# One diffusion layer with a state-space mixer: eigenvalues on half the columns, modulation by halves, states in four blocks

## Chip, core and metric

The kernel runs on one core of one Trainium2 chip. The time is device time of one execution in microseconds (us). Before the change: median 1114.01 of three runs, 1113.48 to 1120.88.

Five engines work beside each other, each in its own order: TensorE (PE; PEld is its weight load), VectorE (DVE), ScalarE (ACT), GpSimd (POOL), and SyncE (SP), which only issues transfers. An instruction waits by semaphores for what it needs, and all that stands behind it on its engine waits with it.

## The reference

One layer, 1024 latent tokens and 256 context tokens, 1024 channels. Everything is float32.

```
m_l, m_c = silu(c) @ ada_w + ada_b, silu(c_ctx) @ ada_w + ada_b      # six vectors of 1024 each
h = rms_norm(x) * (1 + scale) + shift                                # tokens and context, own vectors
# S5: 64 groups of 16 channels, 64 complex states per group, 2 directions
lam_bar = exp(lam * exp(log_step));  b_bar = (lam_bar - 1) / lam * b
h_t = lam_bar * h_{t-1} + b_bar @ u_t;  y_t = Re(c @ h_t)            # over the context, then over the tokens
y = gelu(y_fwd + y_bwd + d * h);  y = y * sigmoid(y @ w_glu + b_glu)
x = x + gate * y
x = x + gate2 * (silu(h2 @ w1) * (h2 @ w3)) @ w2                     # h2: modulated norm of x, hidden 2816
out = rms_norm(x) * norm_final
```

## The kernel before, in words

Eight consecutive tokens form a chunk: 128 chunks of latent tokens and 32 of context. `U` holds tokens transposed, 128 partitions (8 tokens x 16 channels), 64 groups, 160 chunks (`Xc` the 32 of context, `X` the 128 of tokens). The order of the work is written out by hand: the tile library adds the waits, it does not move instructions. Regions of SBUF (`R0`, `RA`, `RU`, `RC[0..3]`, `RXa`, `RXc`) are divided by hand and used several times.

1. **Squares and eigenvalues** (lines 159 to 277). ScalarE squares ten strips, GpSimd adds the two halves of each (line 165), TensorE sums over partitions (166). Beside it VectorE works out exp and sine of the eigenvalues as polynomials, on 128 partitions x 128 columns: 64 states, held twice in the partitions, by 2 directions x 64 groups. `PW` becomes powers 1 to 8 of the eigenvalues, `CP` those times (lam_bar - 1)/lam, by complex products `cmul` (247). `LB` is the table of `CP` in both directions, with signs, copied by ScalarE (276, 277).
2. **Modulation** (`ada1`, `mix_cols`, `u_ctx`, `rs_lat`, `u_lat`). `ada1(k)` multiplies 128 rows of the first 2048 columns of ada_w, from four buffers of 1 MB; `mix_cols` turns the result into columns for all 64 groups. `rs_lat` scales a block of 8 groups by 1/rms on VectorE; `u_lat` modulates it, odd blocks on VectorE, even ones group by group on ScalarE (398); `u_ctx` does the context on GpSimd.
3. **Input matrices.** A half block `hb` is 8 groups in one direction: b = hb // 2, d = hb % 2. `bl_make(hb)` forms two products of 1024 elements of `BXY` and `LB`, on GpSimd for `PMUL`, else on VectorE. `bl_tr` transposes their sum into `Win`: for hb < `NPE` TensorE adds while transposing (343, 344), for the others an accumulating transfer issued by GpSimd adds first (`bl_sum`, 333). `lb_psum` copies parts of `LB` to PSUM, for the VectorE ones. `ada(n)` multiplies tiles of 256 KB of the rest of ada_w, up to tile n of 64; `ada_load` issues their loads on SP, through 16 first and then 8 buffers.
4. **The loop over 16 half blocks** (552 to 583). `sums(hb)`: 32 matrix products and their copies into `ST`, states of all 160 chunks. Behind it in each iteration: `bl_tr(hb + 3)`, `bl_sum(hb + 6)`, `bl_make(hb + 7)`, modulation of block hb + 2, `pair(hb - 1)` (a step of the scan within pairs of chunks, on GpSimd for `PPAIR`). `powers` makes the eigenvalues to the 8th, 16th ... 128th (`SQ`, in PSUM `LQ`). `ctx_low` combines the context's chunks in pairs and fours, quarter by quarter; after the loop `ctx_high` finishes the tree for all at once.
5. **Scan** (`scan`, 641). VectorE: 32 double steps and 63 single ones over all 64 state columns of `ST` (`STE`), with `fill_ops` for two of the four quarters in between; the other two by `fill` on GpSimd.
6. **`run`** (759): a written program for everything beside the scan: A = `ada`, C = output tables by `cl_gen`, K = `k_mats` (kernel matrices; ScalarE copies them at 622 and sends them out), T = `toeplitz` (reads them back), R = `restack` (719, ScalarE copies states for TensorE; the first one is R0), P and Y = products and their copies, F = `fill`, L, G, B, M, Z smaller ones.
7. From line 799 on: the rest of the outputs, the GLU, and the feed-forward network on TensorE.

All of VectorE's and GpSimd's elementwise operations of two tensors stand in the profile under the helper's line 70.

Of the kernel before, what the change touches and what calls it, by code (L numbers as in the profile page):

```python
# [17 lines left out]
P = 128  # L18
# [19 lines left out]
def s5_ffn_kernel(tc, a, out):  # L38
# [3 lines left out]
    with ctx:  # L42
# [67 lines left out]
        ST = view(RA, 0.5, [160, 2, 2, 32])  # L110
        STE = view(RA, 0.5, [160, 2, G])
# [18 lines left out]
        lamp = view(RA, 0, [3, P])  # L130
# [5 lines left out]
        ctxT = view(RA, 40, [G, 32])  # L136
# [6 lines left out]
        stage = [view(RA, 48 + 8 * i, [2048]) for i in range(4)]  # L143
        adaw = a["ada_w"]
        for k in range(4):
            SY.dma_start(stage[k], adaw[k * P:(k + 1) * P, 0:2048])


        def t_(i):
            return view(RA, 1.5 + 0.5 * i, [P])  # L150
# [10 lines left out]
        for i in range(10):  # L161
            src = X[:, 8 * i:8 * i + 8] if i < 8 else ctxT[:, 32 * i - 256:32 * i - 224]
            jk, po = junk[i % 2], psx if i < 8 else psc
            S.activation(jk.rearrange("p a b -> p (a b)").rearrange("p (g c) -> p g c", c=src.shape[2]), src, AF.Square)
            tt(jk[:, 0], jk[:, 0], jk[:, 1], ADD, E)
            PE.matmul(po.rearrange("p g c -> p (g c)"), blk, jk[:, 0], start=i % 8 == 0, stop=i in (7, 9))
# [57 lines left out]
        PW = view(RXa, 0, [8, 2, P])  # L224
        CP = view(RA, 12, [T, 2, P])
# [3 lines left out]
        cmt = view(RXc, 0, [512])  # L229
        yb = LTb[:, 0:256].rearrange("p (r n) -> p r n", r=2)  # L230
        rsp, rcp, colp = LTb[:, 256:384], LTb[:, 384:416], LTb[:, 384:512].rearrange("p (b g) -> p b g", b=2)
# [15 lines left out]
        def cmul(o, x):  # L247

            m = x.shape[1]
            a_, b_ = (t[:, :256 * m].rearrange("p (m r n) -> p m r n", m=m, r=2) for t in (LTa, cmt))  # L250
# [11 lines left out]
        cmul(CP[:, 2:4], CP[:, 0:2])  # L262
        V.tensor_reduce(rsx, psx.rearrange("p g c -> p c g"), AX.X, ADD)
        V.tensor_reduce(rsc, psc.rearrange("p g c -> p c g"), AX.X, ADD)
        S.activation(rsb, rsb, AF.Sqrt, bias=epsc[:, 0:1], scale=1.0 / D)
        cmul(PW[:, 2:3], PW[:, 0:1])
        V.tensor_copy(yb, PW[:, 3])
        cmul(CP[:, 4:6], CP[:, 0:2])
        V.reciprocal(rsp, rsx)
        V.reciprocal(rcp, rsc)  # L270
        cmul(CP[:, 6:8], CP[:, 2:4])
        LB = view(RC[2], 8, [2, T, P])
        for d in range(2):
            sl = slice(64 * d, 64 * d + 64)
            cp_ = CP[:, ::-1, :, sl] if d == 0 else CP[:, :, :, sl]
            S.copy(LB[:, 0, :, sl], cp_[:, :, 0])
            S.activation(LB[:, 1, :, sl], cp_[:, :, 1], AF.Copy, scale=sgn[:, 0:1])

        LH = view(RXc, 0, [2, 3, G])
        SQ = [LS[:, 0], view(RXc, 2, [3, G]), LH[:, 0], LH[:, 1], LS[:, 1]]  # L280

        def powers():

            for gp in range(2):
                o = LS[64 * gp:64 * gp + 64, 0]
                v = PW[64 * gp:64 * gp + 64, 7].rearrange("p r (d g) -> p r d g", d=2)[:, :, :, gp::2]
                S.copy(o[:, 0::2].rearrange("p r (d g) -> p r d g", d=2), v)
                S.activation(o[:, 1].rearrange("p (d g) -> p d g", d=2), v[:, 1], AF.Copy, scale=-1.0)
            tq = view(RXc, 3, [2, G])
            for p in range(4):  # L290
                i_, o = SQ[p], SQ[p + 1]
                if p < 2:
                    V.tensor_copy(LQ[p], i_)
                j_ = LQ[p] if p < 2 else i_
                tt(tq, i_[:, 0:2], j_[:, 0::2], MUL)
                stt(o[:, 1], i_[:, 0], -2.0, j_[:, 2], MUL, MUL)
                stt(o[:, 2], i_[:, 0], 2.0, j_[:, 2], MUL, MUL)
                tt(o[:, 0], tq[:, 0], tq[:, 1], ADD)
# [4 lines left out]
        BL2 = [view(r, kb, [8, T, HC]) for r, kb in ((RC[1], 12), (RXc, 4), (RC[3], 4), (RA, 24), (RA, 28), (RA, 32))]  # L303
# [18 lines left out]
        def lb_psum():  # L322

            for n, hb in enumerate((4, 6, 7, 9, 11, 12, 14)):
                bank, o = ((LTa, 384), (tq, 256), (tq, 384), (lbt, 0), (lbt, 128), (lbt, 256), (lbt, 384))[n]
# [28 lines left out]
        def ada1(k):  # L354
            st = stage[k % 4]
            if k >= 4:
                SY.dma_start(st, adaw[k * P:(k + 1) * P, 0:2048])
            for i in range(4):
                PE.matmul(prow[32 * i:32 * i + 2], scs[:, k], st[:, i * 512:(i + 1) * 512], start=k == 0, stop=k == 7,
                          tile_position=(0, 32 * i))  # L360

        def mix_cols():
            cb = LTa[:, 0:32].rearrange("p (r b j) -> p r b j", r=2, b=2)
            mx = view(RXc, 1, [2, 2, G])
            r4 = view(RXc, 2, [4, P])
            S.copy(r4, prow.rearrange("p (m n) -> p m n", m=4))
            pt = pw()
            for m in range(4):
                PE.transpose(pt[:, m], r4[:, m], ident)
            for r in range(2):  # L370
                tt(cb[:, r].rearrange("p b (j m) -> p b j m", m=4),
                   pt.rearrange("p m (b j q) -> p b j m q", b=2, j=2)[:, :, :, :, r],
                   modb[:, 0:2].rearrange("p b (j m) -> p b j m", m=4), ADD)
            stt(cb[:, :, 1], cb[:, :, 1], 1.0, bc(nrm[:, 0], 1, 2), ADD, MUL)
            tt(mx.rearrange("p r b (j g) -> p (r b j) g", g=T), bc(cb.rearrange("p r b j -> p (r b j)"), 2, T), bc(msk, 1, 32), MUL)
            pcol = pw([2, 2, G])
            PE.matmul(pcol, sel, mx, start=True, stop=True)
            PE.matmul(colp, sel, mx[:, 0], start=True, stop=True)
            S.copy(cols, pcol)
# [11 lines left out]
        def u_lat(b):  # L391
            gs = slice(8 * b, 8 * b + 8)
            if b % 2:
                tt(X[:, gs], X[:, gs], bc(colp[:, 1, gs], 2, P), MUL)
                tt(X[:, gs], X[:, gs], bc(colp[:, 0, gs], 2, P), ADD)
            else:
                for g in range(8 * b, 8 * b + 8):
                    S.activation(X[:, g], X[:, g], AF.Identity, bias=cols[:, 0, 0, g:g + 1], scale=cols[:, 0, 1, g:g + 1])


        NA = 16
        stg = [view(RA, i, [512]) for i in (20, 22, 0, 2, 4, 6, 8, 10, 40, 42, 44, 46, 12, 14, 16, 18)] + [view(RC[2], 8 * (1 - i // 4) + 2 * (i % 4), [512]) for i in range(8)]
# [21 lines left out]
        tt(Xc, ctxT, bc(rcp, 1, G), MUL)  # L424
        for k in range(8):
            ada1(k)
        SY.dma_start(BXY[:, 1], a["bxy"][:, 1])
        ada_load(NA)
        bl_make(0)
        bl_make(1)  # L430
        cmul(PW[:, 7:8], PW[:, 3:4])
        rs_lat(0)
        mix_cols()
        tq = pA.tile([P, 512], F32, tag="r3", name="tq")
        lbt = pA.tile([P, 512], F32, tag="r4", name="lbt")
        u_ctx(0)
        rs_lat(1)
        u_lat(0)
        bl_tr(0)
        bl_tr(1)  # L440
        ada(NA // 2, NA)
        lb_psum()
        bl_make(2)
        u_ctx(1)
        u_lat(1)
        bl_make(3)
        bl_tr(2)
        bl_sum(3)
        ada(NA, NA)
# [949 lines left out]
```

## Time and profile before

| | |
|---|---|
| median of 3 runs | 1114.01 us |
| the profiled execution, its own time | 1120.2 us |
| its span | 1118.4 us |
| TensorE busy | 995.1 us, 89% |
| VectorE | 826.2 us, 74% |
| GpSimd | 647.1 us, 58% |
| ScalarE | 414.4 us, 37% |
| first matrix product of the loop's `sums` | 68.4 us |
| first operation of the scan | 149.7 us |
| first restack | 205.0 us |

The span is the time between the first and the last instruction; the profiled execution's own time lies 1.8 us over it, and 6.2 us over the median. Times in the profile count from the span's start. "Busy" is the sum of instruction times without overlap; an engine that is not busy waits, and the bracket behind a row of the timeline says how long and for whom. The matrix products are pipelined, so their single durations overlap. Rows of a product in float32 count two instructions for each call, transposes one.

### The profile page before, as it was taken

What the parts mean: (1) busy time and instruction counts of PE and PEld (TensorE: products, weight loads), DVE (VectorE), ACT (ScalarE), POOL (GpSimd) and SP (SyncE); (2) the same over time, 40 slices, a digit from 0 to 9 for tenths busy, and PEclk for the clock granted to TensorE, in tenths of its full rate; (3) what the DMA queues carried; (4) which work ended last, traced back from release to release, by engine and by line L of the source; (5) the groups of instructions that cost most, each with busy time, mean ns of one, the idle gap of its engine ahead of it and who ended that gap; (6) DMA issues with size and microseconds to landing.
All of it is one profiled execution on the core that took longest, in us unless ns stands there. A gap on an engine that the chain in (4) does not pass through costs nothing.

```text
span 1118.4 us, 16588 instructions
## 1 busy us (share of the span) xinstructions
PE 995.1 (89%) x6104; PEld 804.1 (72%) x6104; DVE 826.2 (74%) x1690; ACT 414.4 (37%) x868; POOL 647.1 (58%) x503
## 2 busy tenths in 40 slices
PE   4687896746969999879999999999999999999997
PEld 1266622636869997667888888888888888888885
DVE  8979899981777787998666766666666666666657
ACT  4267721734834465222222222222222222222236
POOL 4379787865382353865555555555555555555563
PEclk9698997767999999899999999999999999999999
DMA  9956787754421201101111111111111111111114
GB/s 349 343 105 124 193 259 214 174 112 102 152 74 41 76 1 57 57 19 57 57 57 50 32 35 55 57 57 57 57 57 57 57 57 57 57 56 56 37 41 151
DMA packets 51457, 103.64 MB, mean 93 GB/s; under 512 B 4272, under 2 KB 25008, under 8 KB 49328
## 3 DMA queue, kind: packets, MB, share of 16 engines
q1 hardware_dynamic: 43456, 85.67, 23.1%
q0 software_dynamic: 3600, 13.11, 6.3%
q10 hardware_dynamic: 4320, 3.81, 1.1%
q8 instruction: 48, 0.79, 0.3%
q14 instruction: 33, 0.27, 0.1%
HBM read 83.30 MB, written 6.16 MB: 80 GB/s over the span
## 4 chain that ended last, share of the span: by engine, by line
PE 63%; DVE 20%; ACT 5%; DMA 4%; issue 2%; POOL 1%; ACTq 0%; DVEq 0%; SPq 0%; POOLq 0%
PE pu L1109 10%; PE pu L1108 10%; PE pu L1107 10%; DVE ru L70 6%; PE pd L1107 6%; PE pd L1108 6%; PE pd L1109 6%; DVE ra L70 4%; DVE rxa L70 3%; DMA ra<-kd 2%; PE pw L467 2%; PE pe L873 2%; PE pe L872 2%; PE pe L874 2%; PE pw L737 1%
## 5 line engine op out<-in xcount | busy, mean ns | idle before, releaser
L70 POOL TENSOR_TENSOR c<-rxc,c 128x512 fp32r<-128x512 f32 x128 | 169.9, 1342 | 184.6 <-ACT c L1053 175.8
L70 DVE TENSOR_TENSOR ru<-pd,ru 128x512 f32<-128x512 f32 x336 | 227.0, 690 | 2.3 <-PE pd L1109 2.3
L1108 PE MATMUL pu<-ra,c 128*128 128x512 f32 x432 | 168.2, 389 | 0.6 <-DVE ra L70 0.6
L1109 PE MATMUL pu<-ra,c 128*128 128x512 f32 x432 | 168.3, 390 | 0.3 <-POOL c L70 0.3
L1107 PE MATMUL pu<-ra,c 128*128 128x512 f32 x432 | 168.3, 390 | 0.3 <-ACT ra L1053 0.3
L1053 ACT CAST c<-rxc 128x512 fp32r<-128x512 f32 x128 | 76.7, 617 | 185.6 <-POOL rxc L70 107.2
L1107 PE MATMUL pd<-c 128*128 128x512 f32 x336 | 133.3, 397 | 10.9 <-DVE ru L70 10.9
L1108 PE MATMUL pd<-c 128*128 128x512 f32 x336 | 132.5, 394 | 0.0
L1109 PE MATMUL pd<-c 128*128 128x512 f32 x336 | 132.2, 393 | 0.0
L70 DVE TENSOR_TENSOR ru<-pu,ru 128x512 f32<-128x512 f32 x84 | 57.9, 689 | 87.4 <-PE pu L1109 52.6
L70 POOL TENSOR_TENSOR c<-ru,c 128x1024 fp32r<-128x1024 f32 x22 | 53.3, 2424 | 85.9 <-ACT c L851 77.1
L1109 PEld LDWEIGHTS pu<-ra,c 128*128 128x128 f32 x432 | 81.1, 188 | 17.9 <-POOL c L70 1.2
L1108 PEld LDWEIGHTS pu<-ra,c 128*128 128x128 f32 x432 | 81.1, 188 | 17.7 <-POOL c L70 0.9
L1107 PEld LDWEIGHTS pu<-ra,c 128*128 128x128 f32 x432 | 81.1, 188 | 17.5 <-ACT ra L1053 0.8
L1107 PEld LDWEIGHTS pd<-c 128*128 128x128 f32 x336 | 64.1, 191 | 26.2 <-DVE ru L70 12.9
L1109 PE MATMUL pu<-c,c 128*128 128x512 f32 x192 | 74.8, 390 | 0.4 <-POOL c L70 0.4
L1107 PE MATMUL pu<-c,c 128*128 128x512 f32 x192 | 74.9, 390 | 0.0
L1108 PE MATMUL pu<-c,c 128*128 128x512 f32 x192 | 74.7, 389 | 0.0
L1109 PEld LDWEIGHTS pd<-c 128*128 128x128 f32 x336 | 64.2, 191 | 13.6
L1108 PEld LDWEIGHTS pd<-c 128*128 128x128 f32 x336 | 64.2, 191 | 13.2
L70 DVE TENSOR_TENSOR ru<-ru,rxa 128x512 f32<-128x512 f32 (+1 forms) x62 | 62.7, 1011 | 6.7 <-ACT ru L1252 2.7
L70 POOL TENSOR_TENSOR c<-rxc,rxa 128x1024 f32<-128x1024 f32 x30 | 62.1, 2130 | 9.1 <-PE pw L540 4.2
(289 smaller groups left out, 2220.7 us busy)
## 6 DMA issues: line engine op xcount, KB each, us to landing
c<-in_ada_w SPq DMA_DIRECT2D x48, 256.0 KB, 4.9
ru<-in_w SPq DMA_DIRECT2D x22, 512.0 KB, 3.6
c<-c POOLq DMA_DIRECT2D x19, 512.0 KB, 5.9
rxc<-in_w SPq DMA_DIRECT2D x38, 256.0 KB, 4.4
rxc<-in_w SPq DMA_DIRECT2D x19, 512.0 KB, 5.1
ra<-in_ada_w SPq DMA_DIRECT2D x8, 1024.0 KB, 9.8
ru<-in_xT SPq DMA_DIRECT2D x4, 1024.0 KB, 6.4
ra<-in_ada_w SPq DMA_DIRECT2D x16, 256.0 KB, 6.0
```

What stands on the lines that cost most here:

```text
L70: eng.tensor_tensor(out=o, in0=x, in1=y, op=op)
L467: PE.matmul(pv[64 * (i % 2):64 * (i % 2) + 64, i // 2], w[:, i, 64 * ri:64 * ri + 64], U[:, 8 * b + 4 * j + i], start=True, stop=True)
L737: PE.matmul(inner[u][:, i], U[:, 4 * u + i, 32:160], kq, start=i == 0, stop=False)
L872: PE.matmul(pz, h_[:, k], wH[:, k], start=n == 0, stop=False)
L873: PE.matmul(pz, h_[:, k], wL[:, k], start=False, stop=False)
L874: PE.matmul(pz, l_[:, k], wH[:, k], start=False, stop=n == 7)
L1053: S.copy(o[0], x)
L1107: PE.matmul(pu, wh, bh, start=start, stop=False)
L1108: PE.matmul(pu, wh, bl, start=False, stop=False)
L1109: PE.matmul(pu, wl, bh, start=False, stop=stop)
```

## The change

- **Half the columns.** The input `lam` becomes 128 x 3 x 64: a direction in each half of the partitions, where both halves held both. VectorE's eigenvalue operations, `PW` and `CP` have 64 columns. `dup` multiplies with parts of the identity on TensorE and so writes them into both halves of the partitions: for `LB` (four products of 512 columns, copied alternately by ScalarE and VectorE), for the 8th power (`power8`), and for the output tables (`pw_full`, four times, in iterations 5 to 8, into `PWF`). Two complex products of `PW` go from ahead of the loop into iteration 3.
- **Squares.** The addition on GpSimd goes; TensorE takes both halves of each strip, two products instead of one.
- **Modulation by halves.** `ada1(h, k)` takes 512 of the 1024 channels (for shift and scale each); all 16 tiles have a place of their own and are loaded without waiting for one another, half 0 first. `mix_cols` runs for half 0 ahead of the loop and for half 1 in iteration 2. Half 1's products lie ahead of the loop (4) and in iterations 0 and 1.
- **Order ahead of the loop.** Two half blocks instead of three are transposed there; the third goes into iteration 0. Block 0 is modulated half by ScalarE, half by VectorE. Even blocks are modulated by ScalarE in small portions (`UACT`) over iterations 0 to 10.
- **More adding by TensorE** (`NPE` 4 for 3); `PMUL` has 7 entries for 8.
- **ada_w tiles.** 24 buffers first instead of 16. None is multiplied ahead of the loop, 24 in iterations 3 to 9; after the loop 40 follow instead of 48 from iteration 10 on.
- **States in four blocks.** `ST` becomes four separate quarters `STQ`, 20.125 KB apart; `STE` is the view over all.
- **Context tree by blocks.** `ctx_tree` works on one quarter, all levels but the last, in iterations 4 to 15; quarter 0's two lowest levels on GpSimd. After the loop one tree on a quarter of a quarter and `ctx_last`, with all operands for the factors in PSUM (`LQ`), follow.

```diff
+        STB = 20.125
+        STQ = [view(RA, STB * q + 0.125, [160, 2, 2, 8]) for q in range(4)]
+        STE = view(RA, 0, [4, 161, 2, 16]).rearrange("p q c r e -> p c r q e")[:, 1:]
...
-            tt(jk[:, 0], jk[:, 0], jk[:, 1], ADD, E)
-            PE.matmul(po.rearrange("p g c -> p (g c)"), blk, jk[:, 0], start=i % 8 == 0, stop=i in (7, 9))
+            for j in range(2):
+                PE.matmul(po.rearrange("p g c -> p (g c)"), blk, jk[:, j], start=i % 8 == 0 and j == 0, stop=i in (7, 9) and j == 1)
...
+        def ada1(h, k):
+            for b in range(2):
+                i = 2 * b + h
+                PE.matmul(prow[32 * i:32 * i + 2], scs[:, k], stage[h][k][:, b], start=k == 0, stop=k == 7, tile_position=(0, 32 * i))
+        def dup(pt, src):
+            for d in range(2):
+                sl = slice(64 * d, 64 * d + 64)
+                for j in range(2):
+                    PE.matmul(pt[64 * j:64 * j + 64, :, sl], ident[:, sl], src(d), start=True, stop=True)
...
         V.tensor_reduce(rsx, psx.rearrange("p g c -> p c g"), AX.X, ADD)
         V.tensor_reduce(rsc, psc.rearrange("p g c -> p c g"), AX.X, ADD)
         S.activation(rsb, rsb, AF.Sqrt, bias=epsc[:, 0:1], scale=1.0 / D)
...
         cmul(CP[:, 4:6], CP[:, 0:2])
...
         cmul(CP[:, 6:8], CP[:, 2:4])
+        for k in range(3):
+            ada1(0, k)
         LB = view(RC[2], 8, [2, T, P])
+        for n in range(4):
+            i, t0 = n // 2, 4 * (n % 2)
+            pt = pw()
+            dup(pt, lambda d: CP[:, t0:t0 + 4, i] if d else CP[:, ::-1, i][:, t0:t0 + 4])
...
-        PMUL, NPE = (0, 1, 2, 3, 5, 8, 10, 13), 3
+        PMUL, NPE = (0, 2, 5, 6, 8, 10, 13), 4
...
+        lb_psum(1, 3, 4)
         bl_make(0)
         bl_make(1)
+        bl_make(2)
+        V.reciprocal(rsp, rsx)
+        V.reciprocal(rcp, rsc)
+        for k in range(3, 6):
+            ada1(0, k)
+        power8()
         rs_lat(0)
+        tt(Xc, ctxT, bc(rcp, 1, G), MUL)
+        for k in range(6, 8):
+            ada1(0, k)
+        pt = mix_rows()
+        bl_tr(0)
+        mix_cols(0, pt)
+        u_act(0, 0, 4)
+        u_lat(0, 4)
         u_ctx(0)
+        bl_tr(1)
+        bl_make(3)
+        u_ctx(1)
+        for k in range(4):
+            ada1(1, k)
+        SY.dma_start(BXY[:, 0], a["bxy"][:, 2])
+        ada_load(9)
         rs_lat(1)
+        u_lat(1)
+        rs_lat(2)
+        bl_make(4)
+        bl_make(5)
+        bl_sum(4)
...
+        UACT = {0: (2, 0, 2), 1: (2, 2, 5), 2: (2, 5, 8), 3: (4, 0, 2), 4: (4, 2, 4), 5: (4, 4, 6), 6: (4, 6, 8),
+                7: (6, 0, 2), 8: (6, 2, 4), 9: (6, 4, 6), 10: (6, 6, 8)}
+        RSL = {1: 3, 2: 4, 4: 5, 6: 6, 8: 7}
+        CTREE = {4: [(0, [0], 0, 8, E), (0, [0], 8, 16, E), (0, [1], 0, 16, E)], 6: [(0, [2, 3])],
+                 7: [(1, [0], 0, 8)], 8: [(1, [0], 8, 16)], 9: [(1, [1, 2, 3])],
+                 11: [(2, [0], 0, 8)], 12: [(2, [0], 8, 16)], 13: [(2, [1, 2, 3])], 14: [(3, range(4), 0, 8)], 15: [(3, range(4), 8, 12)]}
+        ADA = {3: 4, 4: 8, 5: 12, 6: 16, 8: 20, 9: 24}
...
         for hb in range(16):
             sums(hb)
+            if hb < 2:
+                for k in range(4 + 2 * hb, 6 + 2 * hb):
+                    ada1(1, k)
+                ada_load(12 + 4 * hb)
+            if hb == 2:
+                pt = mix_rows()
             if hb == 0:
+                bl_tr(2)
                 bl_make(6)
                 bl_sum(5)
+                powers()
             if hb < 13:
                 bl_tr(hb + 3)
+            if hb == 2:
+                mix_cols(1, pt)
...
+            if 5 <= hb < 9:
+                pw_full(hb - 5)
+            if hb in ADA:
+                ada(ADA[hb], ADA[hb])
...
         pair(15, E)
-        ctx_low(3, 1)
-        ctx_high()
+        ctx_tree(3, range(4), 12, 16)
+        ctx_last()
...
-        run("A32 C00 A36 C01 A40 C02 A44 C03 A48 A52 A56 A60 A64 K0 K1 L2 C10 C11 M0 M1 C12 T0 T1 T2 T3 C13 F10 F11 G2 B3 B2 K2 K3"
+        run("A40 C00 A44 C01 A48 C02 A52 C03 A56 A60 A64 K0 K1 L2 C10 C11 M0 M1 C12 T0 T1 T2 T3 C13 F10 F11 G2 B3 B2 K2 K3"
```

More of the change, by code (lines that the diff above doesn't have):

```diff
@@ L352, in bl_tr, with mix_rows @@
                 S.copy(o, t1[:, :, s0])
[L354 to L365, printed above, removed]
+        r4, mx = view(RA, 38, [4, P]), view(RA, 40, [2, 2, 32])
+        def mix_rows():
             S.copy(r4, prow.rearrange("p (m n) -> p m n", m=4))
@@ L491, in rots @@
             for a_ in args:
-                rot(*a_, V, (LTb, tq))
+                rot(*a_, V, (LTb, lbt[:, 256:512]))
         ptmp = [view(RXc, 2 + i, [256]) for i in range(2)]
```

267 lines of the change are left out of this document (144 added, 123 removed).

## The prediction

> **What bounds the kernel now.** First the stages. A row of this answer by stretches holds: the stretch, its length, busy us (instructions) of PE, PEld, DVE, ACT, POOL, the granted TensorE clock, the DMA share, GB/s.
>
> ```profile
> span 1118.4 us, 16588 instructions
> ...
> 45.00:68.40 23.40, 18.71 (x136) 14.91 (x136) 18.04 (x29) 11.42 (x27) 22.37 (x15) 0.78 0.54 174
> 68.40:134.00 65.60, 53.32 (x606) 45.57 (x604) 58.67 (x116) 53.83 (x157) 52.29 (x62) 0.95 0.67 141
> ...
> 139.00:149.70 10.70, 9.50 (x25) 2.13 (x24) 10.29 (x19) 1.25 (x3) 9.99 (x6) 1.00 0.77 269
> 149.70:205.00 55.30, 39.10 (x424) 16.06 (x423) 55.03 (x307) 10.94 (x24) 43.63 (x36) 0.79 0.77 221
> 205.00:283.00 78.00, 48.22 (x720) 43.27 (x720) 47.14 (x215) 42.06 (x98) 47.72 (x48) 0.78 0.61 126
> 283.00:1118.40 835.40, 798.97 (x4093) 675.87 (x4088) 591.68 (x883) 278.71 (x538) 454.11 (x320) 0.98 0.17 57
> ```
>
> The last 835.4 us are TensorE's (799 busy) and the diff does not touch them: only what lies ahead can move. In the loop over half blocks (68.4 to 134) four engines are each busy for 52 to 59 of 65.6 us, so no single one is the bound. Then the timelines (start, duration, instruction; in brackets idle time and who ended it): VectorE, ScalarE, TensorE, GpSimd.
>
> ```profile
> 7.41 4.09 DVE L73 SCALAR_TENSOR_TENSOR ra<-ra 128x128 f32<-128x128 f32 x7
> ...
> 28.01 0.28 DVE L73 SCALAR_TENSOR_TENSOR rxa<-ra 128x128 f32<-128x128 f32 x1
> ...
> 37.47 0.68 DVE L264 TENSOR_REDUCE r<-pw 128x32 f32<-128x512 f32 x1
> 38.07 0.42 DVE L70 TENSOR_TENSOR lta<-rxa,ltb 128x256 f32<-128x256 f32 x1
> ...
> 39.26 0.42 DVE L267 COPY ltb<-rxa 128x256 f32<-128x256 f32 x1
> ...
> 72.75 0.34 DVE L73 SCALAR_TENSOR_TENSOR rxc<-r,lta 128x64 f32<-128x64 f32 x2
> ...
> 85.14 0.43 DVE L70 TENSOR_TENSOR ltb<-ra,lta 128x256 f32<-128x256 f32 x1
> ...
> 86.60 2.34 DVE L70 TENSOR_TENSOR c<-c,lbt 128x1024 f32<-128x1024 f32 x2
> ...
> 144.94 2.18 DVE L70 TENSOR_TENSOR ltb<-ra,r 128x128 f32<-128x128 f32 x1
> ...
> 149.69 0.29 DVE L70 TENSOR_TENSOR ltb<-ra,lta 128x128 f32<-128x128 f32 x1
> ...
> 249.25 0.29 DVE L70 TENSOR_TENSOR ra<-ltc,ra 128x128 f32<-128x128 f32 x1
> ```
>
> ```profile
> 7.62 2.00 ACT L164 ACTIVATE c<-ru 128x1024 f32<-128x1024 f32 x2 [3.00 <-DMA ru<-in_xT]
> ...
> 46.52 0.72 ACT L277 ACTIVATE c<-ra,r 128x512 f32<-128x512 f32 x1
> ...
> 185.43 0.36 ACT L622 COPY r<-kt 128x240 f32<-128x240 f32 x1 [20.60 <-PE kt L621]
> ...
> 205.01 6.98 ACT L719 COPY ra<-ra 64x256 f32<-64x256 f32 x16 [1.69 <-DVE ltc L70]
> ```
>
> ```profile
> 10.12 3.78 PE L166 MATMUL pw<-c,r 128*128 128x512 f32 x4 [10.12 <-POOL c L70]
> ...
> 27.54 1.13 PE L166 MATMUL pw<-c,r 128*128 128x512 f32 x2 [0.55 <-POOL c L70]
> ...
> 28.59 3.62 PE L359 MATMUL prow<-ra,r 128*2 128x512 f32 x32
> ...
> 52.64 0.63 PE L344 MATMUL pw<-r,ra 128*128 128x128 f32 x2
> ...
> 56.20 0.39 PE L344 MATMUL pw<-r,ra 128*128 128x128 f32 x2
> ...
> 60.99 1.90 PE L420 MATMUL pm<-ra,r 128*2 128x512 f32 x16
> ...
> 68.42 2.40 PE L467 MATMUL pw<-ru,c 128*64 128x160 f32 x32
> ...
> 78.14 1.09 PE L346 MATMUL pw<-r,c 128*128 128x128 f32 x8
> ...
> 129.02 6.74 PE L467 MATMUL pw<-ru,c 128*64 128x160 f32 x96
> ...
> 146.45 3.70 PE L540 MATMUL pw<-c,r 128*128 128x512 f32 x8
> ...
> 164.14 1.88 PE L420 MATMUL pm<-c,r 128*2 128x512 f32 x12
> ...
> 182.56 1.76 PE L420 MATMUL pm<-c,r 128*2 128x512 f32 x5 [0.80 <-DMA c<-in_ada_w]
> ```
>
> ```profile
> 45.56 2.02 POOL L70 TENSOR_TENSOR c<-c,c 128x1024 f32<-128x1024 f32 x1 [18.08 <-ACT c L276]
> ...
> 78.62 0.85 POOL L333 DMA_DIRECT2D c<-c  x1 [7.42 <-PE pw L467]
> ...
> 97.84 1.29 POOL L70 TENSOR_TENSOR rxc<-ra,r 128x256 f32<-128x256 f32 x2
> ...
> 139.01 9.98 POOL L70 TENSOR_TENSOR c<-rxc,rxa 128x1024 f32<-128x1024 f32 x5
> ...
> 180.30 0.87 POOL L543 DMA_DIRECT2D c<-c  x1 [0.30 <-POOL c L70]
> ```
>
> And from the page's DMA issues (last figure: us to landing):
>
> ```profile
> c<-c POOLq DMA_DIRECT2D x19, 512.0 KB, 5.9
> ```
>
> Three stations carry the argument: the table LB complete (46.52 + 0.72 = 47.2), the last sums on TensorE (129.02 + 6.74 = 135.8), the first restack on ScalarE (205.0). The scan is not what ends before the third. VectorE does 307 operations in 55.0 us there, 0.18 each; the 32 double steps and fills that the restack needs are some 200, so 149.7 + 36 = 186, and 19 us are to spare. What ends late is the row at 185.43: ScalarE sat 20.6 us until TensorE's kernel matrices, and those stand behind the last ada_w tiles, the last of which waits for a DMA (182.56). From 185.4 to 205.0 ScalarE walks through its own queue.
>
> **The change part by part.**
>
> *Eigenvalues.* 71 operations shrink to 64 columns. Pairs of such run at 0.34 / 2 = 0.17, against 4.09 / 7 = 0.58 now: 12 us from about 4.7 on, then some 6 us of products, so VectorE is at the sums of squares by 23. But these now take two TensorE calls per strip, the addition on GpSimd being gone. A call of 512 columns costs 3.70 / 4 = 0.93 in a row (x8 are two instructions each), 1.13 alone, 1.89 for the first two (3.78). From 8.6 (first square: 7.62 + 1.0) that is 3.8 + 18 x 0.93 = 20.5, to 29.1 (to 32.7 at 1.13). So VectorE waits some 6 us of its gain away, and reduces (0.68) and makes two products (1.2 each by 38.07 to 39.26): 32.2. Doubling is 16 calls of 256 columns, two column halves side by side (the sums' 16 calls of 160 columns take 2.40, 0.15 each, where 160/512 of 0.93 would be 0.29): 16 x 0.23 = 3.7, plus a copy: **LB complete at 36.8 instead of 47.2, 10.4 earlier** (bounds: 6.8 and 13).
>
> On the 0.58: against the 0.28 of 28.01, where GpSimd was idle, it shows VectorE waiting beside GpSimd's additions. The Trainium skill (SBUF — State Buffer, Who interferes with whom) states that a VectorE instruction with two SBUF inputs and a GpSimd instruction exclude each other for whole instructions. By that rule the 0.17 holds; if the stretch stayed, 71 x 0.5 would bring VectorE to the reduction at 46 and nothing would be gained here. The 144.94 row agrees (2.18, GpSimd busy, where 0.29 is usual).
>
> *Up to the first sums.* Now 68.4 - 47.2 = 21. After, VectorE has 9 us to do ahead of the half modulation (the product for power 8 0.9, a make 2.3 (86.60, half of 2.34 twice), reciprocals 1.3, a scaling 1.15, the contexts 2.3, small ones 1), in which TensorE does the rest of the half-0 rows and transposes block 0 (sixteen calls of 128 columns, 16 x 0.23 = 3.7). Then columns, products and copies 2.9, block 1's 3.7, four k of the second half 8 x 0.46 = 3.7: 36.8 + 19.3 = first sums at **56.1, 12 earlier**. The weights are hidden: by 28.59 as many bytes have landed now (four tiles run without a wait), and the half-0 tiles are wanted only from 29 on. If TensorE goes slow in its gaps as at 52.64 (0.63 beside the 0.39 of 56.20), it is 3 us more. The Trainium skill (TensorE: Matmul & The Clock Gate, Part 1: The HAM clock gate) has the clock halved after some 3.4 us of idleness; by it the denser queue here stays fast, and the 3 us fall away.
>
> *The loop* gets what was ahead of it. TensorE, over its 53.3: block 2's doubled transposes 3.7, block 3's 3.7 for 1.1, four k of ada 3.7, modulation 0.9, 24 ada_w tiles (1.90 / 8 = 0.24) 5.7, the full powers 16 x 0.23 = 3.7: **73.6**. VectorE: six makes 2.3 = 13.7, seven pairs (85.14 to 86.60) 1.46 = 10.2, eleven scalings 1.15 = 12.6, trees (256 elements 1.46 each, the levels above taken as 0.9, 0.6, 0.5) 1.5 + 2 x 5.9 + 6, powers, products and small ones 7.5: 63. GpSimd: four makes 17, eight pairs and three tree steps at 4 x 0.65 = 28.6, six contexts 8, eleven issues at 0.85 = 9.4: 63. ScalarE: 53.8 plus copies of 5. Now the fullest engine fills 58.67 / 65.6 = 0.89. With TensorE ahead of the next by ten, I take 0.97: 76 us, last sums at **132.1, 3.7 earlier**; at 1.0 130, at 0.89 139, that is 3 later than now. So most of what is won ahead is spent here.
>
> *Tail before the scan.* 13.9 us from 135.8 to 149.7 become one last tree (2.5) and four operations with PSUM operands (1.2) behind the copies: about 6, and the wait of 144.94 and its like go. VectorE's own sum: 36.8, then 22 ahead of the loop (the 9 above, two makes 4.6, five scalings 5.8, a 2.2 and small ones), 63, 3.7, and its present idle 5.4 + 6.9 + 0.4 = 12.7 from the stretches: scan start 138, 11 earlier. It buys nothing by itself: the restack could follow at 138 + 36 = 174, and comes later.
>
> *After the loop.* 40 instead of 48 ada_w tiles are left; behind the last part of the first C table there were 20, now 12. The 20 take from 164.14 to 184.3: six at 0.3 (x12 in 1.88), which had landed, and 14 at 1.3. Twelve are 6 x 0.3 + 6 x 1.3 = 9.7, 10 less; I take **9** (bounds: 2, if the DMAs keep up at 0.24 a tile, and 10). No more, because of the C products on GpSimd, which start at 139.0 behind the last pair: the last accumulation lands at 180.3 + 0.9 + 5.9 = 187, the second pair of kernel matrices waits for it, and the restack came 18 behind; 9 of these are ScalarE's copies for that pair and the load behind them. So the restack comes at 205.0 - 3.7 - 9 = **192.3**.
>
> *Four blocks.* The addresses of scan, fills and restacks become runs of 16 elements. A pair's 256 elements in runs of four cost 0.43 (85.14), a contiguous product's 0.42 (38.07): nothing. From the restack on, the same work follows: 78.0 + 835.4. The scan's end (249.5) has 33 us to spare before 283.
>
> Sum: 3.7 + 9 = 12.7 off the restack, taken as **12**. The profiled execution took 1120.2 us (span 1118.4 and 1.8 around it), which becomes 1108; it lies 6.2 over the median of 1114.0, so the median becomes **1102**. Own range: from a loop filled to 0.92, ending at 136 (1105), to 1.0 with 10 for the tiles (1098).
>
> **The rivals.** *TensorE takes the place of what is removed* (0.27): the loop stays at 0.89 and ends at 139, the tiles give 9 back: restack 199, median 1108. For it: in-order queues and three engines at 63 beside TensorE's 74. Against: its added calls wait for little. *It all comes through* (0.15): loop at 1.0, the slow clock gone, tiles at their full 10, LB at 34: restack 185, median 1094. Earlier than 177 the scan forbids. *GpSimd's queue gets the upper hand* (0.07): in iteration 4 a pair and three tree steps (10.8) stand ahead of the issue that adds block 11's two products; its transposes stand in TensorE's queue, and everything behind them. From 61 on, when VectorE has made block 4, 38 of its 63 us stand ahead of that issue: 99, landed 106; wanted in iteration 8 at 56 + 76 x 0.62 = 103. Three late is all there is by this count; but if each of blocks 11 to 15 comes late by a pair and a half more, 4.6, that is 23: median 1102 + 23 = 1125. It decides when GpSimd is 10 us later at iteration 4 than counted. For it: 22.37 of 23.4 busy ahead of the loop now. Against: it is idle 13 in the loop. *No gain ahead* (inside the first rival): the squares at 1.13 a call, LB at 40.6, first sums at 60, median 1112.
>
> **How the numbers follow.** Forecast 0.51, rivals 0.27, 0.15, 0.07. One per cent (11 us, about what can be told from no change) lies at 1103: of the forecast 0.31 and all of the fast case lie below it, so faster 0.46; slower 0.07; within 0.47. The range leaves out the slow case and the far end of the fast one: 1092 to 1113.
>
> **What would show it.** LB's last copy near 37, VectorE idle before the reductions from about 23; first sums near 56; TensorE's last sums 130 to 134; scan at 137 to 141; ScalarE's wait before the first kt copy down to about 11; restack 190 to 195, then 913 us as before. Wrong would be: TensorE waiting at the transposes for accumulations (GpSimd), scan steps over 1.05 us, or a restack that waits for the scan.

## The result, and the profile after

| | before | after | ratio, 95% interval |
|---|---|---|---|
| median, us | 1117.45 (1113.48 to 1122.59, 4 runs) | 1153.26 (1151.69 to 1153.81, 4 runs) | 1.0316 [1.0262, 1.0369] |

The change makes the kernel slower by 3.2%. 1102 was forecast, with 1113 as the upper end. (Before has the three runs that the forecast started from, median 1114.01, and a fourth.) The profiled execution of after took 1153.8 us, its span is 1152.0.

| station, us | before | forecast | after |
|---|---|---|---|
| `LB` complete | 47.2 | 36.8 | 35.95 |
| first sums of the loop | 68.4 | 56.1 | 52.6 |
| last sums end | 135.8 | 132.1 | 135.8 |
| scan starts | 149.7 | 138 | 146.9 |
| first copy of kernel matrices (622 before, 708 after) | 185.4 | 172.7 | 174.2 |
| first restack, R0 | 205.0 | 192.3 | **246.75** |
| table load ahead of Gelu (827, now 913) | 285.0 | | 318.4 |
| end of the span | 1118.4 | | 1152.0 |

(Forecast 172.7 is 185.4 less the prediction's 3.7 and 9.) Everything ahead of R0 is earlier than before, or equal. R0 is 41.7 later. This is ScalarE's timeline of after (start, duration, instruction, and in brackets the idle time ahead of it and who ended it):

```profile
174.16 0.36 ACT L708 COPY r<-kt 128x240 f32<-128x240 f32 x1 [8.51 <-PE kt L707]
...
196.63 0.36 ACT L708 COPY r<-kt 128x240 f32<-128x240 f32 x1 [1.29 <-PE kt L707]
...
197.39 0.55 ACTq L573 DMA_DIRECT2D rxc<-in_cxy  x1
246.75 6.89 ACT L805 COPY ra<-ra 64x256 f32<-64x256 f32 x16 [49.76 <-DVE ra L70]
253.67 1.07 ACT L879 COPY ru<-pw 128x512 f32<-128x512 f32 x2
...
318.41 1.28 ACT L913 ACT_TABLE_LOAD   x1
```

ScalarE was through its queue by 198 (197.39 + 0.55), and then waited some 48.8 us for one operation of VectorE (the row's 49.76 count from its last copy, 196.63 + 0.36, and hold the issue of transfers). VectorE's timeline names it: the last addition of the scan ends at 246.43 + 0.29 = 246.72.

```profile
138.16 0.43 DVE L70 TENSOR_TENSOR ltb<-ra,lta 128x256 f32<-128x256 f32 x1
...
139.61 0.29 DVE L70 TENSOR_TENSOR ltb<-ra,lta 128x128 f32<-128x128 f32 x1
...
145.69 0.30 DVE L70 TENSOR_TENSOR ltb<-ra,ltb 128x128 f32<-128x128 f32 x1
...
146.87 0.29 DVE L70 TENSOR_TENSOR ltb<-ra,lta 128x128 f32<-128x128 f32 x1
...
246.43 0.29 DVE L70 TENSOR_TENSOR ra<-ltc,ra 128x128 f32<-128x128 f32 x1
```

The waits of 138 to 300 (engine, what waits, for whom: us in total, times, longest) show that TensorE's products stood behind the same copy, and the stretches (same columns as in the prediction) that TensorE and ScalarE did nothing at all from 205.0 to 246.7:

```profile
ACT ra L805 <- DVE ra L70: 49.8, 1, 49.8
PEld pw L828 <- ACT ra L805: 49.7, 3, 47.7
PE pw L828 <- ACT ra L805: 48.6, 3, 47.4
```

```profile
35.90:52.60 16.70, 16.02 (x115) 9.65 (x111) 15.86 (x25) 6.25 (x16) 12.86 (x10) 1.00 0.53 186
52.60:133.60 81.00, 73.56 (x758) 54.08 (x758) 65.17 (x133) 58.23 (x168) 63.12 (x76) 0.96 0.73 187
138.20:205.00 66.80, 43.97 (x437) 18.59 (x436) 65.87 (x363) 12.10 (x26) 54.40 (x43) 0.82 0.75 213
205.00:246.70 41.70, 0.00 (x0) 0.00 (x0) 39.88 (x186) 0.00 (x0) 13.09 (x12) 0.50 0.25 46
318.00:1152.00 834.00, 797.94 (x4064) 674.30 (x4060) 590.21 (x881) 277.05 (x534) 455.19 (x319) 0.98 0.17 57
```

So the account is: R0 41.7 later; from R0 to the table load 71.7 us (318.41 - 246.75), where before had 80.0 (284.99 - 205.01), VectorE and GpSimd having done 39.88 and 13.09 us of their work during the wait; behind it the same 833 us. 41.7 - 8.3 = 33.4, and the spans differ by 33.6.

The scan is not what R0 reads. In the program as built its wait is for the scan's last addition all the same, and the reason is the place that it **writes**. These lines belong to the change (they are not in the core of the diff above):

```diff
-        KQ = [view(RA, 2 * i, [4, P]) for i in range(4)]
-        HSe = [(RA, 8 + 4 * i) for i in range(2)]
+        KQ = [view(RA, STB * (i // 2) + 2 * (i % 2), [4, P]) for i in range(4)]
+        HSe = [(RA, STB * (2 + i)) for i in range(2)]
```

`HSe` is where the restacks put their result, `KQ` where `toeplitz` reads the kernel matrices back to. Before, both lay at the low end of `RA`, in the context's part of `ST`, which nobody needs after the tree. Now each of the four blocks has such a part at its foot, and `HSe` lies at the feet of blocks 2 and 3. A scan step writes four pieces of 2 x 16 numbers, one in each block, 5152 numbers apart; its last one begins at number 5088 of `RA`, so it covers 32 numbers each from 5088, 10240, 15392 and 20544 on. R0's first copy writes from 10304 on, between the second piece and the third: no number is shared. The library orders the copy behind the last scan step nevertheless. For the place that the copy reads it asks only for a fill of block 0: that is the wait that is left to R0 when its result goes elsewhere, as in the program of experiment 1.

### The profile page after: what moved, and what is told of

It reads as the page before. It is cut to its first block, busy times and chain, and to the rows that moved or that the text cites. A ratio compares the mean times of both kernels' runs of the same rounds, so it can differ in the third digit from the quotient of the medians.

```text
span 1152.0 us, 16907 instructions
## 1 busy us (share of the span) xinstructions
PE 1008.1 (88%) x6228; PEld 811.0 (70%) x6228; DVE 808.6 (70%) x1727; ACT 414.4 (36%) x870; POOL 638.4 (55%) x502
## 4 chain that ended last, share of the span: by engine, by line
PE 65%; DVE 20%; ACT 5%; DMA 4%; POOL 3%; issue 2%; SPq 0%; ACTq 0%; POOLq 0%; DVEq 0%
PE pu L1194 10%; PE pu L1195 10%; PE pu L1193 10%; PE pd L1193 7%; PE pd L1194 7%; PE pd L1195 7%; DVE ra L70 5%; DVE ru L70 5%; DVE rxa L70 3%; DVE ltb L70 2%; PE pw L177 2%; DVE ltc L70 2%; PE pe L959 2%; PE pe L958 2%; PE pe L960 2%
## 5 line engine op out<-in xcount | busy, mean ns | idle before, releaser
L1195 PEld LDWEIGHTS pd<-c 128*128 128x128 f32 x336 | 64.2, 191 | 13.5
L1194 PEld LDWEIGHTS pd<-c 128*128 128x128 f32 x336 | 64.2, 191 | 13.2
```

Of the source, the lines that this page charges most:

```text
L1194: PE.matmul(pu, wh, bl, start=False, stop=False)
L1195: PE.matmul(pu, wl, bh, start=False, stop=stop)
```

## The experiments

Theory A is this: R0 is held by the scan because of where it writes, and nothing else in the change makes it slower. In the expectations other letters stand for the rival that is named beside them. e1 to e4, e5 to e7, and e8 with e9 ran on three different chips; each ratio is against runs of before on the same chip. A station of a profile is from one execution: e1 and e8 are the same program up to R0, and have it at 196.94 and 199.98, so differences of 3 us between stations of two runs say little.

**1. Other places (e1).** The change, with R0's result at the foot of block 0 (a place that ends ahead of the scan's first piece), the others in another region or in parts of block 0 that the scan has passed by then, and the kernel matrices' places moved out of the way:

```diff
-        KQ = [view(RA, STB * (i // 2) + 2 * (i % 2), [4, P]) for i in range(4)]
-        HSe = [(RA, STB * (2 + i)) for i in range(2)]
+        KQ = [view(RA, STB * (1 + i // 2) + 2 * (i % 2), [4, P]) for i in range(4)]
+        HSe = [(RA, 0), (RC[2], 12)] + [(RA, 4), (RA, 8)] * 3
...
-                    hse[i] = hstate(*HSe[len(hse) % 2])
+                    hse[i] = hstate(*HSe[i])
```

(A later use, `HSl[2]`, moves from `2 * STB` to `3 * STB`.)

> The changed kernel with other places alone for what the early restacks write: their 4 KB buffers (at the foot of blocks 2 and 3 in the changed kernel) go to the foot of block 0, into the third table's region and into read-out positions of block 0, the Toeplitz tiles to the foot of blocks 1 and 2. The same operations in the same order on every engine. Theory A (the restack is ordered behind every scan step because its buffer lies between the four pieces that each step writes): ScalarE's first restack goes from 246.7 to 197-200, right behind its own queue; from there some 913 us as in the kernel before, so 1111-1116, unless the fifth restack, which in the kernel before starts at 239.6 with a wait of 0.4 for VectorE's fills, holds it at 236-238: then 1115-1118 and within 1% of the kernel before. Rival B (the restack waits for what it reads: states in blocks are ready only at the scan's end): no change, 1150-1155, restack at 246. Rival C (the blocks' addresses cost on the engines as well): restack near 198, but over 1125.

Measured: 1111.33 us (1108.41 to 1114.64), ratio 0.9947 [0.9929, 0.9965], span 1107.9. ScalarE's timeline:

```profile
171.25 0.36 ACT L708 COPY r<-kt 128x240 f32<-128x240 f32 x1 [8.15 <-PE kt L707]
...
177.44 0.36 ACT L708 COPY r<-kt 128x240 f32<-128x240 f32 x1 [3.32 <-DMA kd<-r]
...
184.79 0.72 ACT L576 ACTIVATE rxc<-rxc,r 128x512 f32<-128x512 f32 x1 [3.90 <-DMA rxc<-in_cxy]
...
193.30 0.36 ACT L708 COPY r<-kt 128x240 f32<-128x240 f32 x1 [4.36 <-DMA kd<-r]
...
195.59 0.36 ACT L708 COPY r<-kt 128x240 f32<-128x240 f32 x1 [1.93 <-DMA kd<-r]
...
196.94 3.42 ACT L805 COPY ra<-ra 64x256 f32<-64x256 f32 x8 [0.99 <-DVE ra L70]
...
228.00 6.78 ACT L805 COPY ra<-ra 64x256 f32<-64x256 f32 x16 [0.40 <-DVE ra L70]
...
272.98 1.28 ACT L913 ACT_TABLE_LOAD   x1
```

R0 comes at 196.94, 49.8 earlier than in after (its 0.99 in brackets is the issue of a transfer ahead of it, 196.35 + 0.55). The arithmetic, its order and every engine's queue are those of after; places alone were worth 41.9 us of the median. From R0 to the end it takes 1107.9 - 196.94 = 911, of the 913 that the prediction took as rigid.

**2. The blocks alone, with the change's places (e2) and with the others (e3).** Before, with only the states in four blocks: `STQ`, `STE` and the addresses of those who use them; `ctx_high` works chunk by chunk there, in seven groups, since one view can't hold it. e2 has the change's two lines, e3 the lines of experiment 1.

```diff
-        ST = view(RA, 0.5, [160, 2, 2, 32])
-        STE = view(RA, 0.5, [160, 2, G])
+        STB = 20.125
+        STQ = [view(RA, STB * q + 0.125, [160, 2, 2, 8]) for q in range(4)]
+        STE = view(RA, 0, [4, 161, 2, 16]).rearrange("p q c r e -> p c r q e")[:, 1:]
```

> The kernel before with one part of the change alone: the states in four blocks, with the places for restacks and Toeplitz tiles that the changed kernel has (the high levels of the context tree, which ran over all columns at once, are seven groups of four operations, one per position). Theory A: restack not before the scan's end, near 249-251 instead of 205, and 8 us given back behind it as in the changed kernel: 1150-1162. Rival B': the loss comes from the new queue orders of the change, not from the blocks: 1112-1125, restack near 205.

> The same kernel before with four blocks, but with the places of the first of these runs. Theory A: the layout by itself costs nothing: restack at 203-207, 1113-1123, the kernel before within 1%. Rival C (addresses cost): scan longer than 101 us or restack copies over 0.44 us each, and 1125 or more.

Measured: e2 1160.28, ratio 1.0384 [1.035, 1.0419]; e3 1115.84, ratio 0.9993 [0.9971, 1.0015]. ScalarE's row of R0 in e2, then in e3:

```profile
251.51 6.90 ACT L731 COPY ra<-ra 64x256 f32<-64x256 f32 x16 [46.62 <-DVE ra L70]
```

```profile
208.49 3.41 ACT L731 COPY ra<-ra 64x256 f32<-64x256 f32 x8 [0.99 <-DVE ltb L70]
```

The blocks with the change's places bring the whole loss by themselves, without one of the other parts; the same blocks with other places cost nothing that can be measured. That also settles the runs of 16 elements: the addresses are free, as forecast. (R0 in e3 is 3.5 behind that of before, 1.5 outside its expectation; the first copy of kernel matrices is late by 2.9 there already, at 188.29.)

**3. A dose (e8).** Experiment 1's kernel with one restack put back into a gap, the fifth, at the foot of block 3. It comes at 228.00 in experiment 1 and the scan ends there at 244.9, so some 17 us of holding were to be expected at that place.

```diff
-        HSe = [(RA, 0), (RC[2], 12)] + [(RA, 4), (RA, 8)] * 3
+        HSe = [(RA, 0), (RC[2], 12)] + [(RA, 4), (RA, 8), (RA, 3 * STB), (RA, 8), (RA, 4), (RA, 8)]
```

> A smaller dose of the same cause, for a price that can be worked out ahead. The run with other places, but the fifth restack's buffer put back to the foot of block 3, in the gap between the pieces that a scan step writes. Nothing it reads changes. Theory A: this restack waits from 228.0 to the scan's end at 244.9, where the cover is 242.1 - 231.4 = 10.7 us (TensorE wants the first half of it at 242.1, behind a wait for Toeplitz tiles, and eight copies take 3.4): so 6 us come through, first table load for the Gelu near 279 instead of 273.0, 1115 to 1120. If a place between the blocks were harmless for a buffer of its own: no change, 228 and 1109 to 1113.

Measured: 1118.04, ratio 1.0001 [0.9979, 1.0023], 6.7 above experiment 1 in the median and 6.0 by the ratios. ScalarE's rows:

```profile
199.98 3.44 ACT L805 COPY ra<-ra 64x256 f32<-64x256 f32 x8 [0.98 <-DVE ra L70]
...
246.46 6.78 ACT L805 COPY ra<-ra 64x256 f32<-64x256 f32 x16 [14.85 <-DVE ra L70]
...
282.63 1.28 ACT L913 ACT_TABLE_LOAD   x1
```

VectorE's last scan addition there:

```profile
246.14 0.29 DVE L70 TENSOR_TENSOR ra<-ltc,ra 128x128 f32<-128x128 f32 x1
```

A second copy, in another block, at another time, waits for the same operation. It comes 18.5 later than in experiment 1, and the table load 9.7 later; 3.0 of each lie ahead of R0, which nothing holds in either run. Counted from R0 the fifth restack is 15.4 later (46.48 behind it, where experiment 1 has 31.06) and the table load 6.6 (82.65 and 76.04), as much as the medians say and as the expectation had worked out. With 1, 2 and 3 theory A is shown.

**4. Is the rest held by the fills? (e4)** Experiment 1's kernel with two of the scan's fills per slot in the single steps, so that they are done sooner, and block 3's upper tree in one go after the loop:

```diff
-            def one():
-                if rest:
-                    rest.pop(0)()
+            def one(n):
+                for f in rest[:n]:
+                    f()
+                del rest[:n]
...
-                step(LQ[0], 31 + k, 32 + k)
+                step(LQ[0], 31 + k, 32 + k, 2)
```

> The first of these runs and two edits more: the last block's context tree over its upper eight columns at once (scan 2 us earlier by 16 operations less), and the fills of block 2 twice as dense between the scan's steps, so that they are done some 15 us sooner, while the scan itself ends no later. If the first run's gain is held up at the fifth restack by those fills, this gives it back: fifth restack 4-8 us earlier than there, and 3-8 us less in all, 1104-1112. If instead something else is last there (GpSimd's C products and its fills of block 3, or the DMAs of the Toeplitz tiles), it stays within 2 us of the first run.

Measured: 1110.61, ratio 0.9935 [0.9915, 0.9955], R0 at 196.42, the fifth restack at 229.33. It did not come earlier (228.00 in experiment 1), so the fills don't hold it: the 3 to 8 us that were expected did not come. What is left is ScalarE's own queue ahead of it; of its 0.40 us of idle time most is the issue of a transfer (227.63 + 0.33 in experiment 1).

**5. Quarter 0's trees on VectorE (e5).** In experiment 1 TensorE waits 4.3 in the loop for the accumulating transfer behind GpSimd's pair and tree steps, the wait of the prediction's slow rival. The trees go to VectorE, all else being experiment 1's kernel:

```diff
-        CTREE = {4: [(0, [0], 0, 8, E), (0, [0], 8, 16, E), (0, [1], 0, 16, E)], 6: [(0, [2, 3])],
+        CTREE = {4: [(0, [0], 0, 8)], 5: [(0, [0], 8, 16)], 6: [(0, [1, 2, 3])],
```

> The run with other places (e1, first sums 51.4, last sums end 134.0, first copy of kernel matrices 171.3, first restack 196.9, 1111.3), with the three context-tree steps of block 0 that stand in GpSimd's queue ahead of an accumulating issue moved to VectorE and spread over iterations 4 to 6. Theory D (GpSimd's queue costs the loop what TensorE waits for that issue, 4.3 us at 108): the wait at the transposes goes, last sums end 129.5 to 132, kernel matrices 167 to 170, and 0 to 4 us less in all, 1107 to 1111. Rival E (VectorE takes the wait over): last sums end 133 to 136, 1110 to 1114.

Measured: 1110.9, ratio 0.9927 [0.9903, 0.9951], last sums end at 136.1 (134.0 in experiment 1). The waits of the loop, first of experiment 1, then of this run:

```profile
PE pw L391 <- DMA c<-c: 4.3, 1, 4.3
```

```profile
PE pw L509 <- ACT rxa L341: 4.8, 1, 4.8
```

The wait that was to go went, and one for ScalarE's copy of the full powers took its place. Taking away GpSimd's lateness alone gave nothing that can be told.

**6. Without the 8 extra ada_w tiles (e6, e9).** Experiment 1 with 16 tiles in the loop and the old string after it, which is what the prediction valued at 9 us:

```diff
-        ADA = {3: 4, 4: 8, 5: 12, 6: 16, 8: 20, 9: 24}
+        ADA = {3: 4, 4: 8, 5: 12, 6: 16}
...
-        run("A40 C00 A44 C01 A48 C02 A52 C03 A56 A60 A64 K0 K1 L2 C10 C11 M0 M1 C12 T0 T1 T2 T3 C13 F10 F11 G2 B3 B2 K2 K3"
+        run("A32 C00 A36 C01 A40 C02 A44 C03 A48 A52 A56 A60 A64 K0 K1 L2 C10 C11 M0 M1 C12 T0 T1 T2 T3 C13 F10 F11 G2 B3 B2 K2 K3"
```

(and 8 buffers fewer). e9 has the one-go tree of e4 as well.

> The run with other places, with 16 instead of 24 ada_w tiles of their own in the loop, and so eight more behind it, as in the kernel before. If the eight tiles are worth what the prediction gave them (9 us behind the loop for about 2 in it): kernel matrices 176 to 180 instead of 171.3, restack 202 to 206, 1116 to 1120. If TensorE does the same work somewhere else and is the bound on both sides: kernel matrices within 2 us of 171.3, 1110 to 1113.

> The run with sixteen tiles and, from the run with early fills, only the last block's tree over its upper eight columns at once (sixteen operations less between the last sums and the scan). The scan and, with it, GpSimd's fills start some 2 us earlier. If those fills hold the end of the stage, 1 to 2 us less than the run with sixteen tiles (1106 to 1110); else the same, 1108 to 1112. Either way it should lie below both kernels.

Measured: e6 1109.94, ratio 0.9912 [0.9885, 0.994], e9 1110.41, ratio 0.9922 [0.9894, 0.995]. ScalarE's rows of e6:

```profile
178.90 0.36 ACT L708 COPY r<-kt 128x240 f32<-128x240 f32 x1 [19.87 <-PE kt L707]
...
198.87 1.29 ACT L805 COPY ra<-ra 64x256 f32<-64x256 f32 x3 [1.74 <-DVE ltc L70]
```

The first copy of kernel matrices comes 7.65 later than in experiment 1 (178.90 against 171.25), about what was forecast for 8 tiles. R0 comes 1.9 later, and the end no later (span 1105.5 against 1107.9); neither of the two expectations came whole. So the 8 tiles that the change moves into the loop buy 8 us at the kernel matrices and nothing at the end. They also cost the loop something: without them its last sums end 3.7 earlier (123.57 + 6.74 = 130.31, where experiment 1 has 133.99). And in experiment 1 four waits for transfers lie between the two stations, 3.32 + 3.90 + 4.36 + 1.93 = 13.5 us in its rows above; in e6 they are 1.00 + 0.96 + 3.27 = 5.2. e9's earlier scan adds nothing to e6, as the second half of its expectation had it.

**7. A late start (e7).** Of the 16 us won ahead of the loop nothing was left at its end. Was the gain not real, or did the loop's added work use it up? Experiment 1's kernel with 8 TensorE calls of 512 columns whose result nobody reads, ahead of the first sums:

```diff
+        for k in range(8):
+            pt = pw([512])
+            PE.matmul(pt, ident, stage[1][k][:, 0], start=True, stop=True)
```

> The run with other places and eight TensorE calls of 512 columns ahead of the first sums, about 7.4 us of work whose result nobody reads. It tells what an earlier first sum is worth. If TensorE's own work is the bound from there on: first sums near 59, last sums end 140 to 142, kernel matrices 177 to 179, 1116 to 1119. If GpSimd, which is busy without a break from 80 on, sets the pace of the loop: last sums end 134 to 137, kernel matrices 171 to 174, 1111 to 1114; then most of the 12 us predicted ahead of the loop could not come through.

Measured: 1122.73, ratio 1.0024 [1.0006, 1.0043]. TensorE's rows:

```profile
53.96 1.10 PE L502 MATMUL pw<-ra,r 128*128 128x512 f32 x2 [2.38 <-DMA ra<-in_ada_w]
55.75 8.01 PE L502 MATMUL pw<-ra,r 128*128 128x512 f32 x14 [0.70 <-DMA ra<-in_ada_w]
63.69 2.39 PE L512 MATMUL pw<-ru,c 128*64 128x160 f32 x32
```

The first sums come at 63.69 instead of 51.35: 12.3 later, more than meant, since the calls also waited for tiles. The last sums end 13.2 later (140.41 + 6.74 = 147.15 against 133.99), R0 12.0 (208.93 against 196.94), and the medians lie 11.4 apart (8.6 by the ratios; the two ran on different chips). So a late start of the loop comes through nearly one to one: the early start was a real gain, and the longer loop spent it.

e1, e4, e5, e6 and e9 all lie between 0.991 and 0.995 of before, with intervals that overlap: each is a little faster than before, by less than 1%, and 3 to 4% faster than after; which of them is best can't be told.

## Why the prediction was wrong, point by point

**The step that failed** is “*Four blocks* ... nothing. From the restack on, the same work follows”. It priced what the four blocks do to addresses: how long an operation with short runs takes. It did not ask what the blocks do to the *places* of the buffers that were cut from `ST`'s dead part, and so to their waits. A price of at most the distance from R0 to the scan's end could have been read from the rows that it quoted: 249.25 against 205.0, 44 us, and “the 32 double steps and fills that the restack needs” assumed that the scan's end is none of its conditions. That price is what came: 41.7. The sentence on the scan's end, “33 us to spare before 283”, rests on the same assumption. “A restack that waits for the scan” stood among the signs of an error, without a chance or a price of its own, and the slow rival was another one.

**Right: the eigenvalues.** The groups of VectorE's instructions (out<-in, count, busy us, mean ns, idle ahead), of before and then of after, both from about 4 us to the end of the polynomials:

```profile
L73 DVE SCALAR_TENSOR_TENSOR ra<-ra 128x128 f32<-128x128 f32 x36 | 17.8, 542 | 0.2
```

```profile
L73 DVE SCALAR_TENSOR_TENSOR ra<-ra 128x64 f32<-128x64 f32 x37 | 6.2, 215 | 0.2
```

6.2 / 37 = 0.17, the value forecast from the pairs. Half the columns would give half of 542, and 215 is less: as the row of 28.01 in the prediction had it, VectorE had waited beside GpSimd's additions, which are gone. The rule of the Trainium skill that the prediction named (SBUF — State Buffer, Who interferes with whom), which the page gives for GpSimd instructions that read SBUF, as those additions do, agrees with this row. VectorE then waited for TensorE's squares, 4.41 + 2.74 = 7.2 (6 forecast), and `LB` was complete at 35.20 + 0.75 = 35.95:

```profile
25.00 0.69 DVE L290 TENSOR_REDUCE r<-pw 128x128 f32<-128x512 f32 x1 [4.41 <-PE pw L177]
28.43 0.69 DVE L291 TENSOR_REDUCE r<-pw 128x32 f32<-128x512 f32 x1 [2.74 <-PE pw L177]
...
35.20 0.75 DVE L77 TENSOR_SCALAR c<-pw,r 128x512 f32<-128x512 f32 x1 [1.03 <-PE pw L280]
```

**Up to the first sums: 3.5 better than forecast** (52.6 for 56.1). The granted clock was 1.00 from 35.9 to 52.6, with TensorE busy 16.02 of 16.70 us; before it was 0.78 from 45.0 to 68.4, with 18.71 of 23.4. That the denser queue stays fast is as the prediction had it by the Trainium skill (TensorE: Matmul & The Clock Gate, Part 1: The HAM clock gate). The 3.4 us of idleness are not what before shows: its granted clock is 1.00 from 31 to 34, 0.97 from 34 to 35 and 0.50 from 35 to 36, behind an idle of 2.39:

```profile
34.60 1.59 PE L359 MATMUL prow<-ra,r 128*2 128x512 f32 x8 [2.39 <-DMA ra<-in_ada_w]
```

**The loop: the work was counted nearly right, its fill too high.** TensorE was busy 73.56 us where 73.6 was counted; both stop 2 us ahead of the end of the last sums, and with these the loop holds 75.8. It took 83.2 (52.60 to 135.77) where 76 was forecast: the fill is 73.56 / 81.0 = 0.91 for the assumed 0.97. Of the 7 us too few, 2 are those left out and 5 the fill. This is the first rival's mechanism, “the loop stays at 0.89”. In-order queues with the three other engines busy for 58 to 65 of 81 us did not pack to 0.97 here, and e5 shows how it resists: where one wait was taken out, the next stood behind it. TensorE's and GpSimd's rows show the one place that the slow rival had counted, issue at 99 and three late; it was issued at 98.76 and TensorE waited 4.25:

```profile
52.60 1.58 PE L509 MATMUL pw<-ru,c 128*64 128x160 f32 x20
...
107.96 1.94 PE L391 MATMUL pw<-r,c 128*128 128x128 f32 x8 [4.25 <-DMA c<-c]
129.03 6.74 PE L509 MATMUL pw<-ru,c 128*64 128x160 f32 x96
```

```profile
98.76 1.74 POOL L378 DMA_DIRECT2D c<-c  x2
```

**The scan starts 9 later than forecast because VectorE was still behind, not because the tail is long.** The last tree and `ctx_last` take 4.3 us where 3.7 were counted:

```profile
142.59 0.29 DVE L70 TENSOR_TENSOR ltb<-ra,lta 128x128 f32<-128x128 f32 x1
```

From there to the scan's first step at 146.87 they run without a break. But when the last sums end, at 135.77, VectorE has a tree of iteration 14, a pair's step (138.16) and a tree of iteration 15 (139.61) still ahead of it. The forecast had let VectorE idle for 6.9 us in the loop, as before; it idled for 15.8 (81.0 - 65.17). As forecast, that start buys nothing by itself: in e9 the scan begins about 4 us earlier than in e1, and the end is the same.

**After the loop: the 9 us came at the kernel matrices, not at R0.** Their first copy is 11.3 earlier than before (174.16), or 14.2 in e1; 12.7 were forecast. R0 would have been free at 198 (ScalarE's queue, above), 7 earlier than before, where the same 12.7 were forecast. The prediction's own second limit binds there. It let the last accumulation of the C products land at 187, with 9 firm behind it: 196, and 192.3 only with the 3.7 that the loop was to end earlier. The loop ended no earlier, GpSimd issued that accumulation at 179.81 (180.30 before), and TensorE waited for it with the second pair of kernel matrices:

```profile
179.81 0.87 POOL L596 DMA_DIRECT2D c<-c  x1 [0.30 <-POOL c L70]
```

```profile
186.03 0.37 PE L699 MATMUL kt<-c,c 128*16 128x112 f32 x2 [2.46 <-DMA c<-c]
```

The other runs fit that. With 24 tiles in the loop (after, e1, e4, e5, e7, e8) R0, or in after the end of ScalarE's queue, comes 18.0 to 19.7 behind this issue and 23.7 to 25.7 behind the first copy of kernel matrices. With 16 tiles (before, e3, e6, e9) it comes 24.5 to 26.6 behind the issue, but 19.6 to 20.5 behind that copy. So two chains lead to R0, and the change traded one for the other; that is read from single executions, and no run moved GpSimd's products alone.

**Right: the rigid end.** From R0 to the end 913 us were taken; after has 905 (1152.0 - 246.75), since work had piled up beside the wait, and e1 911. The stretch from 318 has 797.94 us of TensorE in 834.0, where before had 798.97 in 835.40.

Without the held restack the number is the first rival's. It had R0 at 199 and the median at 1108; e1 has 196.94, and 0.9947 x 1114.0 (the median that the prediction started from) is 1108.1. Its mechanism, the fill, is right, but that the number meets it so closely is in part luck: it had the loop end at 139 and 9 us won behind it, e1 has 134.0, from an earlier start, and 6.3 (8.1 at R0 less 1.8 at the loop's end).

**What stays open.** Why the library sees the write into a gap as touching the scan's pieces, and the read, or the transfers of `toeplitz` into the same kind of gap over all 128 partitions, as apart from them, was not settled by these runs. In e1 a transfer of `toeplitz` writes from number 10304 of `RA` on, just where R0 wrote in after, and waits for no scan step.

## What to carry to other kernels

When a change cuts one tensor into interleaved blocks, list every buffer that lives in its dead parts, and ask of each writer which waits the new place gives it, as carefully as one asks what it reads: a write into the gaps of a strided write that stands ahead of it in the program, on another engine, can be ordered behind it though no number is shared. A long single wait whose releaser produces nothing that the waiting instruction reads is the sign, and moving the buffer is the test. And a gain in front of a loop into which the same change moves work should be forecast at the fill that the loop has now (0.89 before, 0.91 after), with each later station held against the next chain of work behind it.

## What the runs showed that was not expected

- Four pieces, 20 KB apart, in one operand cost VectorE nothing. The scan's groups, before and then after:

```profile
L70 DVE TENSOR_TENSOR ltb<-ra,lta 128x128 f32<-128x128 f32 x95 | 27.8, 293 | 1.1
```

```profile
L70 DVE TENSOR_TENSOR ltb<-ra,lta 128x128 f32<-128x128 f32 x95 | 27.4, 289 | 1.1
```

- An idle of 41.7 us on TensorE and ScalarE does not cost 41.7: 8.3 came back by the table load. ScalarE's shorter hold in e8, 14.85 us, cost 6.6, and there the expectation had said 6.
- A delay of 12.3 us ahead of the loop is not absorbed anywhere up to R0 (12.0), although no engine is busy for more than 0.91 of the loop.
